# Modulation columns in blocks of 2,048 with 128 rows to a load, the first ones by pairs of channel blocks, and routing of three tiles placed one tile earlier

## The chip, the cores and the metric

One NeuronCore of a Trainium2 chip runs the whole kernel. The metric is device time in microseconds (us) from launch to end. PE is the matmul engine (TensorE), PEld its weight loads, DVE is VectorE, ACT is ScalarE, POOL is GpSimd, SP is SyncE, which here only issues DMAs. Everything is fp32 or fp32r (an fp32 pair of high and low part).

## The reference, cut to what matters

A two-layer transformer for 256 tokens x and 256 context tokens, width D = 1024. Each layer starts from a modulation: six vectors of 1,024 per condition (two conditions: c for the tokens, c_ctx for the context), from one matrix product with a weight of 1024 x 6144 per layer.

```
for layer in range(2):
    m = split(silu(cond) @ ada_w[layer] + ada_b[layer], 6)    # for c and for c_ctx
    hx = rmsnorm(x, norm_mix_g) * (1 + m[1]) + m[0]           # the same for ctx
    layer 0: even_mixer (projections, four gated-scan heads, gelu gating, output projection)
    layer 1: mla_mixer  (latent attention)
    x   = x + m[2] * mixer(hx, hc)
    h2  = rmsnorm(x, norm_ffn_g) * (1 + m[4]) + m[3]
    x   = x + m[5] * hier_moe(h2)       # top-1 group, top-2 of 8 experts in it, 32 experts
return rmsnorm(x, final_g)
```

The first two vectors of layer 0 (m[0] and m[1]) are wanted at once; the other ten are wanted later: m[2] to m[5] of layer 0 at the end of its mixer, those of layer 1 after the first MoE.

## The kernel before, in words

The program has four stages one after the other: the even layer (0 to about 393 us of the span), the MoE of layer 0 (to about 890), the odd layer (to about 1085) and the MoE of layer 1. In both MoE stages 192 loads of 1 MB each bring the expert weights through a ring of buffers; PE works through two experts a `step`.

The even layer runs nine matrix products of 512 tokens x 1024 x 512, each of 96 fp32r matmuls of 512 columns on PE (L120 to L122, called from `proj`, `head_proj` and the output loop). In order: a first `proj` (with `modulated` making its input), `head_proj` for heads 0 to 3, each overlapped with the scan `gla` of the head before, two more `proj` (the gating halves, overlapped with the last `gla` and with `gelu`), then the output product in two halves. The first half is the loop at L757 to L765; the second half is the loop over four token tiles at L790 to L807. Each tile of the second half ends with `residual`, `R.tile(t)` (transposes L213, router logits L217, their scaling L218), and `R.rows(t)` (normalised rows, L234 on DVE, L235 on POOL, `split` on ACT and DVE). `R.route` (L240 to L308) picks groups and experts from the logits in some forty small DVE operations; it is called for tiles 0 to 2 and for tile 3, both at t == 3. Between the halves, `R.fold` (L174 to L194) folds modulation vectors into the router weights; it reads them back from DRAM with DMAs that ACT issues (L179).

The modulation is done in 24 chunks of 512 columns (`ada_chunk`), each from two loads of 512 rows x 512 columns, 1 MB each, in rows of 2 KB (`ada_load`, `load`, L330). A chunk is 32 matmuls: 8 row blocks k times 4 column tiles j; column tile j writes 32 output partitions, with 128 columns of the weight moving. fp32 takes two instructions a matmul, so L404 counts 64 a chunk. The bias comes in with 4 more (8 instructions of 128 columns, L412), then one copy (L417) or one DVE operation with the norm gain (L415), and four small DMAs on POOL's queue into the DRAM tensor `mod` (L419). Chunks 0 to 3 (m[0], m[1] of layer 0) are not written to `mod`; they are transposed (L409) into columns `cols` by `first_cols`, two chunks for channel blocks 0 to 3 and two for 4 to 7. The other 20 are strewn over the even layer from the list `todo`: `between` calls `ada_next` after k = 4 and 6 of the first product and after k = 1 and 4 of each later one; the output loop does so at L764; `while adaq` (L808) takes what is left. Each call processes one chunk and issues the loads of the next into `wpb` (two buffers); one chunk is loaded into `wpa` (L786).

The order of instructions within an engine is not the order of the source: a scheduler works it out before the run from modelled times and from the source order as priority, so a chunk of L404 is cut in pieces between other PE work. On the chip each engine takes its queue strictly in order. `nc.sync` is SP's DMA queue, `nc.scalar` ACT's, `nc.gpsimd` POOL's; a DMA that waits for a buffer holds up what stands behind it in its queue.

Of the kernel before, what the change touches and what calls it, by code (L numbers as in the profile page):

```python
# [11 lines left out]
OP = mybir.AluOpType  # L12
# [13 lines left out]
def body(ctx, tc, I, out, dbg=None, stop=None):  # L26
# [310 lines left out]
    def even_layer(HL, main):  # L337
# [6 lines left out]
        with ExitStack() as st:  # L344
# [41 lines left out]
            gain = ap.tile([128, 3, 2, 128], F32, name="gain")  # L386
            V.memset(gain, 0.0)
            gains = {(1, 1): 0, (0, 4): 1, (1, 4): 2}
            for (l, g), i in gains.items():
                src = I["norm_mix_g" if g == 1 else "norm_ffn_g"][l]  # L390
                for j in range(4):
                    nc.gpsimd.dma_start(gain[32 * j:32 * j + 2, i], bass.AP(tensor=src.tensor, offset=src.offset + j * 128,
                                                                            ap=[[0, 2], [512, 2], [1, 128]]))

            def ada_load(l, c, pool):
                return load(I["ada_w"][l][:, c * 512:(c + 1) * 512], pool, nc.gpsimd if l and c >= 12 else nc.sync)

            def ada_chunk(l, c, w, cols=None):

                g, half = divmod(c, 2)  # L400
                pa = P("ad")
                for k in range(KC):
                    for j in range(4):
                        mm(pa[32 * j:32 * j + 32, 0:128], cst[:, k, :], w[k // 4][:, k % 4, j * 128:(j + 1) * 128],  # L404
                           start=k == 0, stop=cols is not None and k == KC - 1, skip_group_check=True)
                r = ap.tile([128, 128], F32, name="ada_r", bufs=2)
                if cols is not None:
                    act(r, pa[:, 0:128], AF.Copy)
                    tp(cols[:, c, :], r, ident)  # L409
                    return  # L410
                for j in range(4):
                    mm(pa[32 * j:32 * j + 2, 0:128], sbi[:, l * 12 + c, :], adab[:, j * 128:(j + 1) * 128],  # L412
                       start=False, stop=True, skip_group_check=True)
                if (l, g) in gains:
                    V.scalar_tensor_tensor(r, pa[:, 0:128], 1.0, gain[:, gains[l, g], half], op0=OP.add, op1=OP.mult)  # L415
                else:
                    act(r, pa[:, 0:128], AF.Copy)  # L417
                for j in range(4):
                    nc.gpsimd.dma_start(mod[l, g, :, half * 512 + j * 128:half * 512 + (j + 1) * 128],  # L419
                                        r[32 * j:32 * j + 2, :])  # L420

            hH = [HL.tile([128, KC, 256], F32R, name=f"hH{c}") for c in range(2)]
            hL = [HL.tile([128, KC, 256], F32R, name=f"hL{c}") for c in range(2)]

            first, w0 = {}, []
            for hf in range(2):
                for g in range(2):
                    first[2 * g + hf] = ada_load(0, 2 * g + hf, wpb if (hf, g) == (1, 0) else rp)
                w0 += load(W_in[hf * 512:(hf + 1) * 512, 2048:2560], wpa)
# [7 lines left out]
            for k in range(KC):  # L437
                p = P("mm")
# [5 lines left out]
                else:  # L444
                    V.tensor_copy(raw[k], p)
            pcol = P("bt", (128, 4, 128))
            cols = [ep.tile([128, 2, 4, 2], F32, name=f"cols{hf}") for hf in range(2)]

            def first_cols(hf):

                for g in range(2):
                    ada_chunk(0, 2 * g + hf, first[2 * g + hf], pcol)
                    V.tensor_tensor(cols[hf][:, g], pcol[:, 2 * g + hf].rearrange("p (b x) -> p b x", x=32)[:, :, 0:2],
# [1017 lines left out]
```

## Time and profile before

| What | Value |
|---|---|
| Median of 3 runs | 1577.54 us (1573.78 to 1579.67) |
| The profiled execution, its own time | 1578.11 us |
| Its span, first to last instruction | 1576.1 us |
| PE busy | 1452.8 us, 92% of the span |
| DVE, ACT, POOL busy | 41%, 27%, 16% |
| Mean DMA rate over the span | 314 GB/s |
| Mean granted clock of PE | 0.968 |

The profile shows one execution. A digit string cuts the span in 40 slices of 39.4 us and gives the busy share in tenths. Busy time of an engine is the union of its instructions; PE's ends are modelled and overlap, so a busy PE is not a PE at its peak. A wait is told with the instruction that ended it. "x64" is a count of instructions, not of source calls.

### The profile page before, as it was taken

What the parts mean: (1) busy time and instruction counts of PE and PEld (TensorE: products, weight loads), DVE (VectorE), ACT (ScalarE), POOL (GpSimd) and SP (SyncE); (2) the same over time, 40 slices, a digit from 0 to 9 for tenths busy, and PEclk for the clock granted to TensorE, in tenths of its full rate; (3) what the DMA queues carried; (4) which work ended last, traced back from release to release, by engine and by line L of the source; (5) the groups of instructions that cost most, each with busy time, mean ns of one, the idle gap of its engine ahead of it and who ended that gap; (6) DMA issues with size and microseconds to landing.
All of it is one profiled execution on the core that took longest, in us unless ns stands there. A gap on an engine that the chain in (4) does not pass through costs nothing. (4 is left out here: it accounts for less than half of the span.)

```text
span 1576.1 us, 21582 instructions
## 1 busy us (share of the span) xinstructions
PE 1452.8 (92%) x8526; PEld 822.1 (52%) x8526; DVE 646.1 (41%) x1476; ACT 432.4 (27%) x984; POOL 249.3 (16%) x272
## 2 busy tenths in 40 slices
PE   6999999998999999999999888997999998988997
PEld 5777777866444444543535356876344433333332
DVE  4555556758214323233322445576232322221323
ACT  4443334523111121121111134454122212211211
POOL 2321212133002202112203301002010200010111
PEclk9999999998999999999999989998999999999999
DMA  9774434885999999999899663125999999999995
GB/s 352 218 248 154 139 130 161 294 321 187 373 409 402 409 403 395 409 401 405 330 401 378 253 253 99 51 100 201 386 409 409 408 409 409 408 409 409 409 409 218
DMA packets 174179, 495.22 MB, mean 314 GB/s; under 512 B 17723, under 2 KB 38636, under 8 KB 174072
## 3 DMA queue, kind: packets, MB, share of 16 engines
q1 hardware_dynamic: 167832, 487.33, 80.9%
q10 hardware_dynamic: 2192, 3.72, 0.6%
q0 software_dynamic: 4048, 2.73, 0.6%
q8 instruction: 70, 1.15, 0.3%
q14 instruction: 37, 0.30, 0.1%
HBM read 492.59 MB, written 1.13 MB: 313 GB/s over the span
## 5 line engine op out<-in xcount | busy, mean ns | idle before, releaser
L921 PE MATMUL gu<-w,xT 128*64 128x512 f32 x2048 | 463.5, 600 | 26.4 <-DMA w<-in_moe_w_gu_dram 21.5
L921 PEld LDWEIGHTS gu<-w,xT 128*64 128x64 f32 x2048 | 150.3, 138 | 327.7 <-issue 272.6
L1037 PE MATMUL dn<-w,hT 128*64 128x512 f32 x960 | 226.7, 608 | 1.9 <-DMA w<-in_moe_w_dn_dram 1.5
L1056 POOL TENSOR_TENSOR xx<-xx,z 128x512 f32<-128x512 f32 x64 | 82.9, 1308 | 775.2 <-DVE z L1055 775.2
L929 DVE COPY hh<-gu 128x256 f32<-128x256 f32 x64 | 27.2, 425 | 373.6 <-ACT he L928 373.6
L1037 PEld LDWEIGHTS dn<-w,hT 128*64 128x64 f32 x960 | 69.0, 139 | 138.4 <-issue 128.9
L928 ACT ACTIVATE he<-gu 128x256 f32<-128x256 f32 x64 | 24.5, 383 | 406.6 <-PE gu L921 406.6
L1052 PE MATMUL ad<-y,PT 128*128 128x512 f32 x360 | 100.0, 417 | 20.0 <-DVE z L1055 19.9
L120 PE MATMUL mm<-WH,hH 128*128 128x512 f32 x288 | 117.1, 409 | 1.2 <-ACT hH L115 1.2
L121 PE MATMUL mm<-WL,hH 128*128 128x512 f32 x288 | 115.2, 401 | 1.4 <-DVE WL L116 1.4
L122 PE MATMUL mm<-WH,hL 128*128 128x512 f32 x288 | 112.2, 399 | 0.0
L1042 DVE SCALAR_TENSOR_TENSOR y<-dn,ws,y 128x512 fp32r<-128x512 f32 x60 | 45.1, 751 | 139.6 <-ACT y L1041 137.6
L1052 PEld LDWEIGHTS ad<-y,PT 128*128 128x128 f32 x360 | 64.7, 192 | 56.3 <-DVE z L1055 29.8
L1041 ACT ACTIVATE y<-dn,ws 128x512 fp32r<-128x512 f32 x60 | 41.2, 687 | 185.8 <-PE dn L1037 181.9
L1055 DVE TENSOR_TENSOR z<-ad,gt 128x512 f32<-128x512 f32 x96 | 65.7, 689 | 62.8 <-POOL xx L1056 38.3
L116 DVE TENSOR_TENSOR WL<-w,WH 128x512 fp32r<-128x512 f32 x76 | 56.6, 752 | 55.2 <-ACT WH L115 54.6
L115 ACT ACTIVATE WH<-w 128x512 fp32r<-128x512 f32 x80 | 48.5, 627 | 109.6 <-PE mm L122 89.0
L404 PE MATMUL ad<-w,cst 128*32 128x128 f32 x1536 | 60.5, 285 | 5.7 <-DMA w<-in_ada_w_dram 5.6
L120 PEld LDWEIGHTS mm<-WH,hH 128*128 128x128 f32 x288 | 55.2, 192 | 17.5 <-issue 4.0
L419 POOL DMA_DIRECT2D mod<-ada_r x80 | 40.4, 512 | 141.6 <-ACT ada_r L417 127.9
L121 PEld LDWEIGHTS mm<-WL,hH 128*128 128x128 f32 x288 | 55.2, 192 | 13.3 <-DVE WL L116 1.5
L122 PEld LDWEIGHTS mm<-WH,hL 128*128 128x128 f32 x288 | 54.1, 189 | 13.0 <-issue 1.6
(439 smaller groups left out, 1946.3 us busy)
## 6 DMA issues: line engine op xcount, KB each, us to landing
w<-in_moe_w_gu_dram SPq DMA_DIRECT2D x256, 1024.0 KB, 16.3
w<-in_moe_w_dn_dram SPq DMA_DIRECT2D x120, 1024.0 KB, 11.5
w<-in_ada_w_dram SPq DMA_DIRECT2D x48, 1024.0 KB, 7.4
w<-in_ev_w_in_dram SPq DMA_DIRECT2D x32, 256.0 KB, 4.3
w<-in_moe_w_dn_dram SPq DMA_DIRECT2D x16, 512.0 KB, 11.3
w<-in_ev_w_in_dram SPq DMA_DIRECT2D x6, 1024.0 KB, 5.0
w<-in_ev_w_out_dram SPq DMA_DIRECT2D x4, 1024.0 KB, 6.8
w<-in_od_w_out_dram SPq DMA_DIRECT2D x4, 1024.0 KB, 5.0
```

Source lines behind the costliest of these rows:

```text
L115: act(H, src, AF.Copy)
L116: (eng or V).tensor_tensor(L, src, H, op=OP.subtract)
L120: mm(out, lh, rh, start=start, stop=False, skip_group_check=True)
L121: mm(out, lh, rl, start=False, stop=False, skip_group_check=True)
L122: return mm(out, ll, rh, start=False, stop=stop, skip_group_check=True)
L404: mm(pa[32 * j:32 * j + 32, 0:128], cst[:, k, :], w[k // 4][:, k % 4, j * 128:(j + 1) * 128], start=k == 0, stop=cols is not None and k == ...
L921: mm(gu[64 * c:64 * c + 64, :], xT[:, k, base:base + CAP], w[:, c], start=k == 0, stop=k == KC - 1)
L1037: mm(py[c][64 * par:64 * par + 64, :], hT[par][:, k // 2, k % 2, :], w_[par][:, k % 2, c * 512:(c + 1) * 512], start=k == 0, stop=k == 3)
L1042: V.scalar_tensor_tensor(y[c][:, 1], py[c], ws, y[c][:, 0], op0=OP.mult, op1=OP.subtract)
L1052: mm(cb, PT[:, t, :], y[c][:, i % 2], start=i == 0, stop=i == 2 * len(pend) - 1)
L1055: V.tensor_tensor(z, cb, gate[t // 2][:, hs_], op=OP.mult)
L1056: nc.gpsimd.tensor_tensor(xs[t][:, hs_], xs[t][:, hs_], z, op=OP.add)
```

## The change

Three parts, all in the even layer.

1. The modulations other than the first two are made in five blocks of 2,048 columns (two vectors each) instead of 20 chunks of 512. A block has four parts (`ada_part`), each of two loads of 128 rows x 2,048 columns (1 MB each, rows of 8 KB). A part is 8 matmuls, 4 column tiles of 512 moving columns for each of 2 row blocks (16 instructions), that go on summing in one PSUM bank over the four parts; the fourth part adds the bias (8 instructions of 512 columns) and makes one copy and four DMAs. There are again 20 parts of 2 MB. `between` calls them after k = 6 of the first product and k = 1, 3 and 6 of each later one.
2. The first two vectors are made in four units of two channel blocks (256 columns of each vector) instead of two of four blocks; each unit has four loads of 512 KB in rows of 1 KB. The normalised transposes (`raw_block`, before L437 to L445) are no longer all ahead of it: blocks 0 to 3 come first, 4 to 7 between the units, and they use the PSUM tag `bt`.
3. `R.route(0, 3)` is called at t == 2 instead of t == 3.

```diff
-            gain = ap.tile([128, 3, 2, 128], F32, name="gain")
+            gain = ap.tile([128, 2, 512], F32, name="gain")
...
+            def first_load(u, pool):
+                ws = []
+                for i in range(2):
+                    w = pool.tile([128, 4, 2, 256], F32, name="w")
+                    for g in range(2):
+                        c0 = g * D + 256 * u
+                        mark["load"] = nc.sync.dma_start(w[:, :, g], I["ada_w"][0][i * 512:(i + 1) * 512, c0:c0 + 256]
+                                                         .rearrange("(k p) n -> p k n", p=128))
+                    ws.append(w)
+                return ws
+            def first_unit(w, pc):
+                pa = P("ad")
                 for k in range(KC):
                     for j in range(4):
+                        mm(pa[32 * j:32 * j + 32, 0:128], cst[:, k, :], w[k // 4][:, k % 4, j // 2, (j % 2) * 128:(j % 2 + 1) * 128],
+                           start=k == 0, stop=k == KC - 1, skip_group_check=True)
...
+                act(r, pa[:, 0:128], AF.Copy)
+                tp(pc, r, ident)
+            def ada_load(l, q, i, pool):
+                ws = []
+                for k in (2 * i, 2 * i + 1):
+                    w = pool.tile([128, 2048], F32, name="w")
+                    mark["load"] = nc.sync.dma_start(w, I["ada_w"][l][k * 128:(k + 1) * 128, q * 2048:(q + 1) * 2048])
+                    ws.append(w)
+                return ws
+            def ada_part(l, q, i, w):
+                if i == 0:
+                    bank[0] = P("ad")
+                pa = bank[0]
+                for kk in range(2):
+                    for j in range(4):
+                        mm(pa[32 * j:32 * j + 32, :], cst[:, 2 * i + kk, :], w[kk][:, j * 512:(j + 1) * 512],
+                           start=i + kk == 0, stop=False, skip_group_check=True)
+                if i < 3:
                     return
                 for j in range(4):
+                    mm(pa[32 * j:32 * j + 2, :], sbi[:, l * 12 + 4 * q + j, :], adab, start=False, stop=True, skip_group_check=True)
+                r = ap.tile([128, 512], F32, name="ada_r", bufs=1)
+                if (l, q) in gains:
+                    p0, n = gains[l, q]
+                    V.scalar_tensor_tensor(r[p0:p0 + 64], pa[p0:p0 + 64], 1.0, gain[p0:p0 + 64, n], op0=OP.add, op1=OP.mult)
+                    act(r[64 - p0:128 - p0], pa[64 - p0:128 - p0], AF.Copy)
                 else:
+                    act(r, pa, AF.Copy)
                 for j in range(4):
+                    nc.gpsimd.dma_start(mod[l, 2 * q + j // 2, :, (j % 2) * 512:(j % 2 + 1) * 512], r[32 * j:32 * j + 2, :])
...
+            w0 = []
+            first = [first_load(0, rp)]
+            w0 += load(W_in[0:512, 2048:2560], wpa)
+            first += [first_load(1, rp), first_load(2, wpb)]
+            w0 += load(W_in[512:1024, 2048:2560], wpa)
+            first.append(first_load(3, rp))
...
             def modulated(k):
-                if k % 4 == 0:
-                    first_cols(k // 4)
+                if k == 0:
+                    for i in range(4):
+                        raw_block(i)
+                    first_cols(0)
+                elif k in (2, 4):
+                    raw_block(k + 2)
+                    raw_block(k + 3)
+                if k % 2 == 0 and k < 6:
+                    first_cols(k // 2 + 1)
...
-            todo = [(0, c) for c in range(4, 12)] + [(1, c) for c in range(12)]
+            todo = [(l, q, i) for l, q in ((0, 1), (0, 2), (1, 0), (1, 1), (1, 2)) for i in range(4)]
...
-                if k in ((4, 6) if first else (1, 4)) and adaq:
+                if k in ((6,) if first else (1, 3, 6)) and adaq:
                     ada_next()
...
-                if t == 3:
+                if t == 2:
                     R.route(0, 3)
+                elif t == 3:
                     R.route(3, 4)
```

## Rows read from the trace of the kernel before

**Rows 1.** The page's slices of PE and of the DMA engines.

```profile
PE   6999999998999999999999888997999998988997
...
DMA  9774434885999999999899663125999999999995
```

**Rows 2.** Stretches 405 to 410 and 430 to 500 us: busy per engine, clock, DMA share, GB/s.

```profile
405.00:410.00 5.00, 5.00 (x26) 1.69 (x24) 0.97 (x4) 0.00 (x0) 0.00 (x0) 1.00 0.72 228
430.00:500.00 70.00, 67.23 (x344) 31.11 (x342) 21.93 (x38) 12.60 (x29) 10.37 (x8) 1.00 1.02 405
```

**Rows 3.** PE's waits from 60 to 342 us: total, times, longest.

```profile
PE ad L404 <- DMA w<-in_ada_w_dram: 4.2, 4, 2.3
```

**Rows 4.** L404 alone by stretch: PE busy (instructions), PEld busy, clock, DMA.

```profile
60.00:287.00 227.00, 31.00 (x768) 21.38 (x768) 0.99 0.53 169
287.00:334.00 47.00, 8.06 (x192) 5.65 (x192) 1.00 0.86 310
```

**Rows 5.** L412 (the bias) alone in the first of these stretches.

```profile
60.00:287.00 227.00, 4.95 (x96) 1.22 (x96) 0.99 0.53 169
```

**Rows 6.** PE's timeline around one chunk that runs almost whole.

```profile
191.23 1.74 PE L404 MATMUL ad<-w,cst 128*32 128x128 f32 x56
192.90 0.40 PE L412 MATMUL ad<-adab,sbi 24*2 24x128 f32 x8
193.22 0.50 PE L120 MATMUL mm<-WH,hH 128*128 128x512 f32 x1
```

**Rows 7.** The chain that ended last: expert products, two column tiles of 64, 512 columns.

```profile
1259.74 13.97 PE gu L921 x64
```

**Rows 8.** PE's timeline before the first product.

```profile
27.67 0.33 PE L409 MATMUL bt<-ident,ada_r 128*128 128x128 f32 x1 [1.76 <-ACT ada_r L408]
...
29.66 0.80 PE L120 MATMUL mm<-WH,hH 128*128 128x512 f32 x1 [0.49 <-ACT hH L115]
```

**Rows 9.** DVE's timeline at the end of the first product.

```profile
59.20 0.69 DVE L518 COPY sg<-mm 128x512 f32<-128x512 f32 x1 [1.98 <-PE mm L122]
```

**Rows 10.** Stretches with loads in rows of 2 KB, then of 512 B (columns as in 2).

```profile
16.00:36.00 20.00, 17.27 (x244) 14.29 (x244) 11.01 (x27) 8.01 (x19) 0.00 (x0) 0.91 1.05 383
144.50:147.50 3.00, 3.00 (x24) 2.23 (x26) 2.29 (x4) 0.88 (x2) 0.00 (x0) 1.00 0.93 266
```

**Rows 11.** Four loads of 256 KB (L477), issued 142.5 to 144.0 us.

```profile
DMA to landing us min/median/max: 3.7/4.3/4.5
```

**Rows 12.** ACT's timeline at the end of the output product's first half.

```profile
330.48 0.28 ACT L417 ACTIVATE ada_r<-ad 128x128 f32<-128x128 f32 x1 [3.25 <-PE ad L412]
```

**Rows 13.** DVE's timeline there.

```profile
335.53 1.12 DVE L187 TENSOR_TENSOR wA<-wr,rcol 128x320 f32<-128x320 f32 x2 [7.75 <-DMA rcol<-mod]
```

**Rows 14.** PE's timeline from there to the second half's first products.

```profile
334.65 1.95 PE L404 MATMUL ad<-w,cst 128*32 128x128 f32 x64
...
342.94 0.60 PE L121 MATMUL mm<-WL,hH 128*128 128x512 f32 x1 [1.37 <-DVE WL L116]
```

**Rows 15.** PE's timeline at the end of the even layer.

```profile
371.18 1.98 PE L217 MATMUL bt<-wA,h2T 128*128 128x40 f32 x16
...
374.04 1.28 PE L404 MATMUL ad<-w,cst 128*32 128x128 f32 x34
...
380.26 1.52 PE L404 MATMUL ad<-w,cst 128*32 128x128 f32 x32 [1.44 <-DMA w<-in_ada_w_dram]
381.71 3.64 PE L217 MATMUL bt<-wA,h2T 128*128 128x40 f32 x16
...
403.19 1.08 PE L921 MATMUL gu<-w,xT 128*64 128x512 f32 x4
```

**Rows 16.** DVE's timeline there.

```profile
380.19 0.26 DVE L218 SCALAR_TENSOR_TENSOR lg<-bt,rs_y,bS 128x40 f32<-128x40 f32 x1
...
385.39 0.26 DVE L218 SCALAR_TENSOR_TENSOR lg<-bt,rs_y,bS 128x40 f32<-128x40 f32 x1 [0.73 <-PE bt L217]
...
392.44 1.22 DVE L861 TENSOR_TENSOR P<-iota,cm 128x1024 fp32r<-128x1024 f32 x1
```

More of the change, by code (lines that the diff above doesn't have):

```diff
@@ L385, in even_layer @@
             nc.gpsimd.dma_start(adab, I["ada_b"].rearrange("l (c n) -> (l c) n", n=512))
-            gain = ap.tile([128, 3, 2, 128], F32, name="gain")
+            gain = ap.tile([128, 2, 512], F32, name="gain")
             V.memset(gain, 0.0)
[L388 to L400, printed above, removed]
+            gains = {(1, 0): (64, 0), (0, 2): (0, 0), (1, 2): (0, 1)}
+            for (l, q), (p0, i) in gains.items():
+                src = I["norm_ffn_g" if q else "norm_mix_g"][l]
+                for j in range(2):
+                    nc.gpsimd.dma_start(gain[p0 + 32 * j:p0 + 32 * j + 2, i], bass.AP(tensor=src.tensor, offset=src.offset + j * 512,
+                                                                                      ap=[[0, 2], [1, 512]]))
+            def first_load(u, pool):
[9 more added lines that the diff above has]
+            def first_unit(w, pc):
                 pa = P("ad")
@@ new lines, in first_unit @@
+                r = ap.tile([128, 512], F32, name="ada_r", bufs=1)[:, 0:128]
+                act(r, pa[:, 0:128], AF.Copy)
[7 more added lines that the diff above has]
+                return ws
@@ L416, in ada_chunk @@
                 else:
-                    act(r, pa[:, 0:128], AF.Copy)
+                    act(r, pa, AF.Copy)
                 for j in range(4):
-                    nc.gpsimd.dma_start(mod[l, g, :, half * 512 + j * 128:half * 512 + (j + 1) * 128],
-                                        r[32 * j:32 * j + 2, :])
+                    nc.gpsimd.dma_start(mod[l, 2 * q + j // 2, :, (j % 2) * 512:(j % 2 + 1) * 512], r[32 * j:32 * j + 2, :])
+            bank = [None]
             hH = [HL.tile([128, KC, 256], F32R, name=f"hH{c}") for c in range(2)]
@@ L423, in even_layer @@
             hL = [HL.tile([128, KC, 256], F32R, name=f"hL{c}") for c in range(2)]
[L425 to L429, printed above, removed]
+            w0 = []
+            first = [first_load(0, rp)]
+            w0 += load(W_in[0:512, 2048:2560], wpa)
+            first += [first_load(1, rp), first_load(2, wpb)]
@@ L436, in even_layer, with raw_block @@
                 V.tensor_scalar(dg[:, t, :], ident, rstd_of(xs[t], D, 1.0 / D, dg0), None, op0=OP.mult)
-            for k in range(KC):
-                p = P("mm")
+            def raw_block(k):
+                p = P("bt")
                 for t in range(4):
```

34 lines of the change are left out of this document (13 added, 21 removed).

## The prediction

> **What bounds the kernel now.** I read the page's slices first. PE is nearly full all along, and the DMA engines are full in two stretches only [rows 1]: slices 11 to 22 and 29 to 40, the two MoE stages. From 40 to 315 us their digits are 3 to 8 while PE's are 9. So the even layer is PE's and each MoE stage the DMA engines'. The reader is to see that nothing in the MoE stages changes, and that all that can change is when the even layer lets the first of them begin.
>
> Then the windows view, to see whether an earlier beginning is worth anything. In 430 to 500 us the DMA share is 1.02 at 405 GB/s: the expert weights set the pace. But in 405 to 410 us the share is 0.72 [rows 2]: the ring of buffers is full and the loads wait until PE, which began its first expert product at 403.19 [rows 15], gives a buffer back. What the even layer gains or loses therefore moves all that follows by as much, and I make the sum on the position of that product.
>
> Then the waits of PE from 60 to 342 us: four waits for modulation weights, 4.2 us together [rows 3]. PE's own work sets the order there, so each us added to PE between 60 and 287 us is a us on the path. Last, the timelines of three places in which PE does wait: the start, the seam between the two halves of the output product, and the end of the layer.
>
> **The change, part by part.**
>
> *A chunk's price now.* In 60 to 287 us, 768 instructions of L404, which are 12 chunks, keep PE busy for 31.00 us, and their bias for 4.95 [rows 4, 5]: 2.99 us a chunk. A chunk that runs nearly whole takes 193.22 - 191.23 = 1.99 [rows 6]. So about 1 us of a chunk's price comes from its being cut up among other products.
>
> *A part's price.* The trace has no product of four column tiles with 512 columns moving. The nearest is the expert product: two column tiles, 512 columns, 64 instructions in 13.97 us [rows 7], 218 ns each. With four tiles side by side, as L404 has them, I estimate half of that, 109 ns: 16 instructions make 1.75 us, and the bias (8 instructions for four parts) 0.22 a part. That is 1.97, the whole chunk's 1.99 again: the columns are the same in number, so the wide tile by itself gains nothing, and only cutting can be saved. Below: 1.97, never cut. Above: 2.99, cut as now. I take 2.5, halfway, since 16 long instructions offer fewer seams than 72 short ones, but the work that cuts in is the same.
>
> *Heads and the two later products, 60 to 287 us: +9 us.* By the new places, heads take 12 parts and the two products 6, 18 in place of 12 chunks: 18 x 2.5 = 45 for 12 x 2.99 = 36. Between 18 x 1.97 = 35.5 (nothing) and 18 x 2.99 = 53.8 (+18). Their copies (5 in place of 20) and their POOL DMAs (20 for 80) hide behind PE as they did. Each part still needs 2 MB, at 405 GB/s some 5.2 us, in two buffers that come free only when the part before is done; behind such a load in SP's queue stand the head weights. Three parts in a stage stand two or three row blocks apart (24 or 36 products) and mostly more, with a scan between.
>
> *The start: -5 us.* First loads of x and ctx (2.1 MB), two chunks (4.2 MB) and 1 MB of W_in now stand before the first product, which starts at 29.66 [rows 8]. After: one unit, so 2.1 MB less, at 383 GB/s [rows 10] 5.5 us. PE's wait of 1.76 for ACT, which was copying weights, may go too: -7.3 at best. Against it, units come in rows of 1 KB. The trace has rows of 2 KB (383 GB/s at share 1.05, so 365 at a full share) and of 512 B (266 at 0.93, so 286) [rows 10]. All 8.4 MB at 286 would take 29.4 us in place of 23: the last unit 6.4 us later, which eats the lead, since the last quarter of the product waits for it. So -7.3 to 0 for the product's end, at 59.2 now [rows 9]; 1 KB lies between the two rates, and raw blocks 4 to 7 fill PE's waits: I take -5. The product holds one modulation piece at its end before and after.
>
> The Trainium skill ("DMA: Bandwidth & Descriptors") asks for loads of at least 1 MiB (section Measured (HBM→SBUF, 128 partitions, SWDGE, issued from GpSimd)) and gives one DMA about 2.0 us plus bytes / 436e3 (section Anatomy of one DMA — SWDGE (gpsimd) path). If loads followed one another by that formula, 16 of 512 KB would take, by estimate, 51 us where 8 of 1 MB take 35, and the kernel would come out 16 us later than my sum. The trace speaks against loads following one another.
>
> *The output product's first half and the seam: -6 us.* In 287 to 334 us three chunks run, 192 instructions of L404 [rows 4], 8.06 and some 1.2 of bias, 9.3 us. One part remains (2.5). At the seam, ACT stood 3.25 us before a chunk's copy at 330.48, waiting for PE's bias [rows 12], and the DMA that reads `mod` back for the fold is behind that copy in ACT's queue; DVE then stood 7.75 for it to land [rows 13]. PE filled the time with two whole chunks from 334.65 on and still waited 1.37 for the split weights at 342.94 [rows 14]. With no chunk there, the fold's DMA goes at least 3.25 sooner; the cover for the two chunks was free, so taking them out gives nothing itself. At most the seam moves by the 6.8 us taken from PE in front. I take 6: the third chunk's pieces stood ahead of the transposes that end the gating. Bounds 3 to 7.
>
> *The end: -5 us.* The last tile's logits were ready at 385.39 on DVE, waiting for L217 [rows 16]. Ahead of that L217 on PE stood a piece of a chunk at 374.04 (with its bias 1.5 us), a wait of 1.44 for weights and a piece of 1.45 [rows 15]: 4.4 us that go. It also took 3.64 where that of another tile took 1.98 [rows 15]. From the third tile's logits (380.19) to the one-hots (392.44) DVE has 12 us of work, both routes and a split [rows 16]. Routing three tiles earlier lets that start before the last tile's logits. If DVE's 12 us were simply full, only the 1.5 us would be won; if all went, 7. I take 5. Late next would be the last tile's normalised rows (DVE, POOL, ACT, DVE in turn), which now share DVE with a route that has priority. No DMA is moved with the route; the expert loads behind the last chunks on SP go sooner, but into a ring that is full before PE starts anyway.
>
> *Sum.* -5 + 9 - 6 - 5 = -7. From the profiled execution's 1578.1: 1571 us; its time is 0.6 above the median of 1577.5, so the median is about as good a start.
>
> **Rivals.**
>
> *A, the sum*, 1571, with its own range 1562 to 1578. Chance 0.52.
>
> *B, uncut parts.* If the scheduler leaves parts whole, the heads cost nothing more: 1571 - 9 = 1562. For it: one chunk in the heads does run whole [rows 6]. Against: most are cut, or 12 would not cost 36. It comes out lower still if the start gives 7. Chance 0.14.
>
> *C, the shift gives all back.* Parts cost what chunks cost: +18 in place of +9, so 1580. Six pieces move from places where PE waited anyway (seam, end) into the stretch in which it doesn't, and nothing is earned by that. Chance 0.13. Here too belongs that the expert loads are behind at the start and swallow the lead, 1578; against it the 0.72 [rows 2]; 0.04.
>
> *D, PE waits for modulation weights in the heads: slower.* Three parts a stage on one pair of buffers, each load let go only by the part before. Now 4 waits take 4.2 us over the 12 chunks [rows 3], the longest 2.3. If each of 18 parts waited 1.2 more, that would be +22: 1593. It decides from 0.85 us a part, where the 15 us between my sum and slower by 0.5% are used up. For it: SP's strict order and 6 MB in place of 4 a stage. Against: from 60 to 287 us the DMA share is 0.53 at 169 GB/s [rows 4]. Chance 0.12.
>
> *E, first loads one after another*: the 16 half-size loads of the start, if each took its landing time alone. Four loads of 256 KB issued over 1.5 us landed 3.7 to 4.5 us after their issue [rows 11]; one behind another they would have needed four times 3.7. By the shortest landing 16 loads would take 59 us, some 30 more than the bytes, of which PE's other work hides half: about 1586. Chance 0.05. The skill's formula above gives 1587 for the same course.
>
> **How the numbers follow.** 0.5% is 7.9 us, about what a measurement of this kernel can tell from no change; faster is below 1569.6, slower above 1585.4. My point lies just inside. Of A's 0.52, about 0.32 falls below 1569.6, since four terms each uncertain by some 4 us spread the sum by about 8; all of B is faster: 0.46. The rest of A, and C, are the same: 0.37. D and E are slower: 0.17. Reaching down through B to 1558 and up past C to 1585 leaves out D and E and little else, under 2 in 10.
>
> **What would show each step.** Parts: L404's successor busy per part in the heads, 2.5 (B: 2.0; C: 3.0); the stretch from the first product's end to the last gating product's, longer by about 9. Start: first product near 24 to 25, its end near 54. Seam: no modulation work between the halves, the fold's DMA issued before 330, the second half starting about 3 to 6 sooner after the first. End: no modulation work behind the second half's products; from the third tile's logits to the one-hots below 10 us. D: waits of the modulation products for their DMA above 20 us in total. The MoE stages should be as long as before. The prediction is wrong if the first expert product moves by 7 and the end doesn't, or if the heads' stretch moves by more than 18.

## The result and the profile after

The changed kernel takes 1586.38 us (median of 7, 1583.88 to 1593.51) where the kernel before takes 1577.54 in the same comparison: ratio 1.008, 95% interval 1.0051 to 1.011. It is slower by 0.8% by that ratio (the two medians alone stand 0.56% apart); 1571 was forecast, in a range of 1558 to 1585. The profiled execution spans 1584.6 us in place of 1576.1, so its own difference is +8.5.

The page's slices of the changed kernel, first row PE, then the clock granted to PE, then the DMA engines, say that the balance is the old one ([rows 1]): the two MoE stages are the DMA engines', the even layer is PE's.

```profile
PE   7999999986799999999999888997999989988997
...
PEclk9999999997899999999999899997999999999999
DMA  9885455853799999999899863225999999999995
```

So the reckoning is made as in the prediction, on positions in the even layer. I cut it at four instructions that both kernels have: the first matmul of head 0, the last of the seventh product, the third tile's logits on DVE, the one-hots on DVE (the matrix P with which the gather picks its rows).

| stretch | before | after | difference | forecast |
|---|---|---|---|---|
| start, to head 0's first matmul | 63.45 | 58.90 | -4.6 | -5 |
| heads and the two later products | 237.35 | 247.75 | +10.4 | +9 |
| output's first half and seam, to the third tile's logits | 79.39 | 77.04 | -2.4 | -6 |
| end, to the one-hots | 12.25 | 18.46 | +6.2 | -5 |
| gather, to the first expert product | 10.75 | 10.63 | -0.1 | 0 |
| all behind it | 1172.9 | 1171.8 | -1.1 | 0 |

The differences add up to +8.4, the span's +8.5. Two lines are right, one gave less than half, and the end went the other way by 11 us. That one is most of the error. (Of the end's -5, the 1.5 for the piece at 374.04 in [rows 15] belong by their place to the line above: that piece stood ahead of the third tile's logits.)

PE's timeline of the changed kernel at its first product and at these cuts (start, length, instruction, what it waited for; [rows 8, 15] answer to the first and last of them), then the kernel before at the two cuts that its rows don't show:

```profile
25.66 0.50 PE L120 MATMUL mm<-WH,hH 128*128 128x512 f32 x1
...
58.90 0.50 PE L120 MATMUL mm<-WH,hH 128*128 128x512 f32 x1
...
306.65 0.39 PE L122 MATMUL mm<-WH,hL 128*128 128x512 f32 x1
...
412.78 1.08 PE L963 MATMUL gu<-w,xT 128*64 128x512 f32 x4
```

```profile
63.45 0.39 PE L120 MATMUL mm<-WH,hH 128*128 128x512 f32 x1
...
300.80 0.39 PE L122 MATMUL mm<-WH,hL 128*128 128x512 f32 x1
```

**The end.** PE's timeline of the changed kernel behind the second half's products, then DVE's ([rows 15, 16] answer to them):

```profile
382.60 1.05 PE L217 MATMUL bt<-wA,h2T 128*128 128x40 f32 x4
392.30 0.21 PE L282 MATMUL bt<-Mb,before 128*128 128x32 bf16 x1 [8.64 <-DVE Mb L274]
392.40 1.94 PE L213 MATMUL bt<-ident,w 128*128 128x128 f32 x8
...
394.31 3.61 PE L217 MATMUL bt<-wA,h2T 128*128 128x40 f32 x16
```

```profile
383.69 0.26 DVE L218 SCALAR_TENSOR_TENSOR lg<-bt,rs_y,bS 128x40 f32<-128x40 f32 x1 [1.07 <-PE bt L217]
...
397.97 0.26 DVE L218 SCALAR_TENSOR_TENSOR lg<-bt,rs_y,bS 128x40 f32<-128x40 f32 x1 [3.19 <-PE bt L217]
...
402.15 1.23 DVE L903 TENSOR_TENSOR P<-iota,cm 128x1024 fp32r<-128x1024 f32 x1
```

Read the order in PE's queue, not the durations. L282 is the rank product of the route of tiles 0 to 2 (it counts each token's place in its expert's list); it needs their one-hot mask Mb, the end of a chain on DVE. It now stands ahead of L213 and L217, the last tile's transposes and logits, which need nothing from that route. PE stands 8.64 us at it with the last tile's work behind it. So its logits come at 397.97, 12.6 us later than in [rows 16], and the second route begins only then: the two routes, which shared DVE before, run one behind the other, with DVE idle for 3.19 us between.

**The heads.** The windows of the two kernels over that stretch (sum of PE, weight loads, DVE, ACT and POOL busy, clock, DMA share, GB/s), first the kernel before, then the changed one; then the changed one's modulation products L435 and bias L440 alone:

```profile
63.50:300.80 237.30, 232.40 (x1925) 180.04 (x1924) 135.95 (x290) 92.02 (x177) 57.43 (x76) 0.99 0.56 182
```

```profile
58.90:306.60 247.70, 246.85 (x1376) 163.75 (x1373) 135.63 (x274) 95.14 (x173) 41.24 (x40) 1.00 0.62 213
...
58.90:306.60 247.70, 48.17 (x284) 7.82 (x280) 1.00 0.62 213
...
58.90:306.60 247.70, 4.14 (x32) 0.41 (x32) 1.00 0.62 213
```

A part is 16 instructions. Four of the 284 belong to a piece that starts at 57.91 and reach in with their modelled ends only; 280 are 17.5 parts: (48.17 + 4.14) / 17.5 = 2.99 us a part, just what a chunk cost, 2.99 [rows 4, 5]. Why so much, PE's timeline shows, around a part that runs whole, around one that is cut within a row, and around half a part with the bias behind it:

```profile
123.13 1.92 PE L435 MATMUL ad<-w,cst 128*32 128x512 f32 x16
124.98 0.50 PE L120 MATMUL mm<-WH,hH 128*128 128x512 f32 x1
...
148.07 1.04 PE L435 MATMUL ad<-w,cst 128*32 128x512 f32 x2
149.04 0.66 PE L721 MATMUL bt<-ident,o 128*128 128x128 f32 x4
...
150.96 1.92 PE L435 MATMUL ad<-w,cst 128*32 128x512 f32 x14
152.81 0.50 PE L122 MATMUL mm<-WH,hL 128*128 128x512 f32 x1
...
323.21 1.06 PE L435 MATMUL ad<-w,cst 128*32 128x512 f32 x8
324.21 1.03 PE L440 MATMUL ad<-adab,sbi 24*2 24x512 f32 x8
```

Sixteen records took 1.85 from start to next start; 2 took 0.97 and the other 14 again 1.85; 8 took 1.00. A pair of records is one matmul in one column tile, eight records are one row of four tiles side by side, and a lone tile takes as long as all four. The Trainium skill ("TensorE: Matmul & The Clock Gate", section Measured speedup vs the span model) says the same from the other end: a pack lasts about one matmul and some 4 ns for each further tile; here 0.97 for one tile and 1.00 for eight records. So a cut within a row costs a whole row more, 0.97, where a whole row of a chunk takes 0.24 ([rows 6]: 56 records, seven rows, in 1.67).

**The first half.** PE's waits of the changed kernel from 58.9 to 306.6 us, then from 306.6 to 345, then of the kernel before from 300.8 to 334.3 (total, times, longest); [rows 3] answers to the first:

```profile
PE ad L435 <- DMA w<-in_ada_w_dram: 0.8, 2, 0.5
...
PE mm L120 <- ACT hH L115: 4.4, 2, 3.3
PE bt L792 <- DVE gv L789: 1.8, 1, 1.8
...
PE ad L404 <- DMA w<-in_ada_w_dram: 0.5, 1, 0.5
PE mm L120 <- ACT hH L115: 0.4, 1, 0.4
```

The waits for modulation weights are nearly gone. But in the output product's first half PE now waits 6.2 us for the gated half of the input, where the kernel before waited 0.4 for it and 0.5 for weights. Its timeline there with the gating products, those of the kernel before, and the window behind the wait:

```profile
317.95 1.95 PE L775 MATMUL bt<-gv,wsT 128*128 128x128 f32 x16
...
322.65 0.63 PE L792 MATMUL bt<-ident,gv 128*128 128x128 f32 x4 [1.76 <-DVE gv L789]
...
329.13 0.79 PE L120 MATMUL mm<-WH,hH 128*128 128x512 f32 x1 [3.30 <-ACT hH L115]
```

```profile
301.03 1.95 PE L734 MATMUL bt<-gv,wsT 128*128 128x128 f32 x16
```

```profile
329.00:335.00 6.00, 5.87 (x16) 4.70 (x17) 3.41 (x7) 1.51 (x5) 0.62 (x2) 0.50 0.23 89
```

The gating products of the last two tiles (L775) stand at 317.95, behind four row blocks of the output product; in the kernel before they ran at 301.03, right behind the seventh product. And after the wait the granted clock is 0.50 for 6 us, its lower level: the 96 products of this half take 24.8 us in place of 22.9.

### The profile page after: what moved, and what is told of

The parts are those of the page before. It is cut to its first block, busy times and chain, and to the rows that moved or that the text cites. A ratio compares the mean times of both kernels' runs of the same rounds, so it can differ in the third digit from the quotient of the medians.

```text
span 1584.6 us, 19309 instructions
## 1 busy us (share of the span) xinstructions
PE 1452.2 (92%) x7446; PEld 791.6 (50%) x7446; DVE 650.4 (41%) x1475; ACT 433.3 (27%) x975; POOL 218.1 (14%) x206
## 5 line engine op out<-in xcount | busy, mean ns | idle before, releaser
L120 PEld LDWEIGHTS mm<-WH,hH 128*128 128x128 f32 x288 | 54.7, 190 | 35.0 <-issue 12.1
L122 PEld LDWEIGHTS mm<-WH,hL 128*128 128x128 f32 x288 | 54.4, 190 | 14.6 <-issue 3.1
L928 PE MATMUL ad<-P,hH 128*128 128x256 f32 x256 | 52.9, 289 | 1.8 <-DVE P L903 1.8
L435 PE MATMUL ad<-w,cst 128*32 128x512 f32 x320 | 53.2, 603 | 0.8 <-DMA w<-in_ada_w_dram 0.8
## 6 DMA issues: line engine op xcount, KB each, us to landing
w<-in_ev_w_in_dram SPq DMA_DIRECT2D x6, 1024.0 KB, 10.4
```

What stands on the lines that cost most here:

```text
L120: mm(out, lh, rh, start=start, stop=False, skip_group_check=True)
L122: return mm(out, ll, rh, start=False, stop=stop, skip_group_check=True)
L435: mm(pa[32 * j:32 * j + 32, :], cst[:, 2 * i + kk, :], w[kk][:, j * 512:(j + 1) * 512], start=i + kk == 0, stop=False, skip_group_check=True)
L928: mm(px[:, j, :], hs[t][:, part, 128 * k:128 * k + 128], P[:, t, :], start=i == 0, stop=i == 2 * NT - 1)
```

## The experiments

Each kernel was timed beside the kernel before on one chip, in groups (e1 to e4, e5 to e8, e9 to e12, e13 and e14) on a chip each. A profiled execution can lie some us off the median of its kernel (that of the route back is 8.5 below it and the fastest of its six runs), so totals are read from the ratios and the causes from positions within the traces.

| kernel | ratio to before | 95% interval | first expert product | third tile's logits to one-hots |
|---|---|---|---|---|
| changed kernel | 1.0080 | 1.0051 to 1.011 | +9.6 | 18.5 |
| e1 route back | 1.0044 | 1.0031 to 1.0058 | +3.1 | 12.3 |
| e2 route alone | 1.0026 | 1.0010 to 1.0042 | +3.0 | 16.0 |
| e3 rank late | 1.0043 | 1.0025 to 1.0061 | +3.5 | 12.3 |
| e4 pairs alone | 0.9981 | 0.9963 to 0.9999 | -3.1 | 11.4 |
| e5 places alone | 1.0027 | 1.0009 to 1.0046 | -0.1 | 12.3 |
| e6 width, old places | 1.0111 | 1.0088 to 1.0134 | +12.3 | 14.6 |
| e7 whole rows, new places | 1.0021 | 1.0004 to 1.0039 | -0.2 | 12.1 |
| e8 whole rows, old places | 1.0020 | 1.0003 to 1.0038 | +1.7 | 15.0 |
| e9 pairs and places | 1.0018 | 0.9998 to 1.0037 | +3.3 | 12.3 |
| e10 weights late | 1.0006 | 0.9986 to 1.0025 | -1.2 | 11.4 |
| e11 addition on DVE | 0.9969 | 0.9955 to 0.9982 | -8.8 | 10.9 |
| e12 both | 0.9972 | 0.9954 to 0.9991 | -7.6 | 9.4 |
| e13 gate buffers | 1.0025 | 1.0007 to 1.0043 | +3.2 | 12.3 |
| e14 all mended | 0.9981 | 0.9964 to 0.9997 | -7.4 | 12.6 |

**The route, from three sides.** e1 takes it back in the changed kernel, e2 puts it alone into the kernel before, e3 keeps its DVE work early and moves only its rank products behind the last tile:

```
                 rstd = R.tile(t)
-                if t == 2:
+                if t == 3:
                     R.route(0, 3)
-                elif t == 3:
                     R.route(3, 4)
```

```
                 if t == 2:
-                    R.route(0, 3)
+                    R.route(0, 3, rank=False)
                 elif t == 3:
+                    R.rank(0, 3)
                     R.route(3, 4)
```

> The changed kernel with the route of tiles 0 to 2 back behind the last tile's logits. Theory Q (PE's fixed order): in the changed kernel the rank product L282 of tiles 0 to 2, which waits for DVE's one-hots, stands in PE's queue ahead of the last tile's transposes L213 and logits L217, and so DVE's first route delays the last tile's logits. Then this kernel has the last tile's logits 8 to 13 us sooner than the changed one, the one-hots of the gather 6 to 10 us sooner, and it takes 1576 to 1580 us in place of 1586. Rival V (DVE is simply full from the third tile's logits to the one-hots, and what was lost is a slower DVE beside POOL and half clock on PE): the logits come sooner but the one-hots don't, and the time stays within 2 us of 1586.

> The kernel before with the earlier route alone. Theory Q: the rank product again stands ahead of the last tile's transposes, so the last tile's logits (385.4 in the kernel before) come 8 to 12 us later and the time is 1582 to 1587 us, nearly the whole loss of the changed kernel. Rival V: both routes are the same work on DVE in any order, no change beyond 2 us. Prediction's step: 3 to 7 us faster, 1571 to 1575.

> The changed kernel with the route of tiles 0 to 2 still at the earlier place on DVE, and only its rank products (L282, L284) and the one addition that reads them moved behind the last tile's logits. Theory Q: PE's order is mended and DVE has its first route done sooner, so the last tile's logits come as early as in the kernel with the route back, and the one-hots 0 to 4 us earlier than there: 1573 to 1580 us. Rival V (DVE's share is what delays): as slow as the changed kernel, 1584 to 1588, since DVE's order is the same.

PE's timeline with the route back, then DVE's busy time from the third tile's logits to the one-hots in e1 and in e3 (columns as in the windows above), then PE's and DVE's timelines with the route alone:

```profile
383.20 3.47 PE L217 MATMUL bt<-wA,h2T 128*128 128x40 f32 x16
392.04 0.29 PE L282 MATMUL bt<-Mb,before 128*128 128x32 bf16 x2 [5.37 <-DVE Mb L274]
```

```profile
382.60:394.90 12.30, 4.81 (x30) 4.48 (x28) 12.23 (x66) 2.36 (x6) 3.40 (x3) 0.50 0.27 85
...
383.80:396.10 12.30, 4.82 (x30) 4.49 (x28) 12.23 (x66) 2.36 (x6) 3.40 (x3) 0.50 0.27 85
```

```profile
385.72 0.19 PE L282 MATMUL bt<-Mb,before 128*128 128x32 bf16 x1 [0.83 <-DVE Mb L274]
385.75 1.95 PE L213 MATMUL bt<-ident,w 128*128 128x128 f32 x8
...
387.67 3.61 PE L217 MATMUL bt<-wA,h2T 128*128 128x40 f32 x16
...
391.32 0.26 DVE L218 SCALAR_TENSOR_TENSOR lg<-bt,rs_y,bS 128x40 f32<-128x40 f32 x1 [3.02 <-PE bt L217]
```

The queue's order decides (theory Q). With the last tile's L217 back in front of L282 its logits come at 386.9 in place of 398.0, and 6.1 us of the stretch are back, all that it had lost. The route alone costs 3.8 us there, since two chunks cover a part of PE's wait, and 0.26% in the time; its 1581.5 us lie just under the range, and its last logits came 5.9 us later, not 8 to 12. The mended order in e3 is worth as much as e1, and no more: DVE's earlier start gives nothing, because DVE is busy for 12.23 of the 12.30 us in both. That is the case for which the prediction had kept its lower bound.

The totals say less than the positions. e1's 1584.9 missed its 1576 to 1580 and e3's 1583.8 its 1573 to 1580; by its median alone e1 even lies where rival V had it, within 2 us of 1586. What excludes V is the trace: the one-hots came 7.3 us sooner. In the whole time the ratio moved by 0.36%, 5.7 us, with intervals that overlap; the clearest measure of the order is e2's 0.26%, whose interval does not reach 1.

**The start alone.** e4 is the kernel before with the diff's parts for the first units, nothing else.

> The kernel before with only the first modulations by pairs of channel blocks. Theory S (the start gives less than the prediction's 5, because the second half of the first product waits for its later units): first product 4 us sooner, its end 1 to 3 us sooner, and the same through to the end: 1574.5 to 1577. Rival: the whole 5 arrives at the end, 1572.5. Rival: the heads take it all back, 1577 to 1579.

Head 0's first matmul comes 4.0 us sooner, the first expert product 3.1, the time is 0.19% less. Its 1574.4 us lie just below theory S's range and above the rival's 1572.5, though more of the lead was there at head 0 than the 1 to 3 us of S. In e10, e11 and e12, which have the same first loads, the start gave 3.3, 4.5 and 2.4. It varies by as much without the pairs: e2, which begins as the kernel before does, has head 0 at 61.17, 2.3 us sooner (its granted clock from 30 to 60 us was 1.00, that of the kernel before 0.96), and e5, with one place fewer in the first product and no pairs, at 59.09.

**Places, width and cuts.** e5 and e9 change the places and keep chunks of 512 columns, e9 with the pairs; e6 keeps the wide parts and takes the places back; e7 and e8 put a part's eight matmuls at the scheduler's highest priority, so that nothing else cuts into a row (e8 at the old places).

```
-                if k in ((4, 6) if first else (1, 4)) and adaq:
+                if k in ((6,) if first else (1, 3, 6)) and adaq:
```

```
+                with tc.high_priority():
                     for kk in range(2):
                         for j in range(4):
                             mm(pa[32 * j:32 * j + 32, :], cst[:, 2 * i + kk, :], w[kk][:, j * 512:(j + 1) * 512],
```

> The kernel before, its chunks of 512 columns kept, at the changed kernel's places alone (one in the first product, three in each later stage). Theory W (the heads lose by the wide part, since 16 of its records are only two rows of four column tiles, and a piece that holds one tile of a row takes as long as the whole row): chunks at the new places cost at most 2.99 us each as before, so 18 for 12 is +13 to +18 before the output product, the seam gives 6 to 8 back and the end, with no chunk there, 3 to 5: 1576 to 1584 us, and the modulation work of the heads is no dearer by the piece than before. Rival P (the places are all of the loss, width none): the output product begins 12 to 16 us later, as in the changed kernel, and the time is that of the changed kernel with the route back, 1.0044 of before.

> The kernel before with the first modulations by pairs and the new places, its chunks of 512 columns and its route kept: the change without its wide parts and without the earlier route. If the terms add up, it is the 4 us of the pairs on top of the places alone (1.0027): first expert product 3 to 5 us sooner than in the kernel before, time 0.998 to 1.002 of before, 1573 to 1579 us. Rival (the pairs' 4 us are lost where the places put a third piece into every stage): no faster than the places alone, 1.0027.

> The changed kernel (wide parts, first modulations by pairs) with the places of before and the route back. Theory W: 12 parts of 2.7 to 2.8 us stand where 12 chunks of 2.8 to 3.0 did, so the heads change by -3 to 0, the start gives 3.8, and 7 parts are left for the output product and the end as 8 chunks were: 1571 to 1576 us. Rival P2 (wide parts cost more in themselves, wherever they stand): 1577 or above.

> The changed kernel with the route back and the eight matmuls of a part at the scheduler's highest priority, so that no other product cuts into a row of four column tiles; places as changed. Theory W: a row costs 1.0 us alone and two rows 1.85, so 17 parts cost 32 to 35 us and not 48, the output product begins 8 to 14 us sooner than in the changed kernel with the route back, and the time is 1566 to 1576. Rival P: the number of parts sets the price, not their cuts; the same time as with the route back. Rival D of the prediction: whole parts stand in front of products that are ready and PE waits for their weights, more than 10 us in total, 1585 or above.

> Wide parts, pairs, the route back, places of before, and the rows of four kept whole by priority. Theory W: 12 parts in the heads cost 24 in place of 33 to 36 us, the start gives 3.8, seam and end stay nearly as before: 1562 to 1569. If the seam and the end matter more than the heads, it is no faster than the kernel with whole rows at the new places.

The modulation products and their bias with whole rows, over the stretch from head 0 to the seventh product (columns as before):

```profile
60.50:302.80 242.30, 38.82 (x300) 6.12 (x296) 1.00 0.67 228
...
60.50:302.80 242.30, 6.16 (x32) 0.56 (x32) 1.00 0.67 228
```

Of the 300 instructions 296 begin in the stretch, 18.5 parts, at 44.98 us 2.43 each in place of 2.99, and more of them: the cuts within rows cost about 0.55 us a part. Chunks at the new places (e5) cost 3.00, as at the old ones, and e5's time lies where theory W had it, though not by W's path: only 15.7 chunks fell into the stretch, which grew by 4.7 us (242.0 for 237.35), and the output product began 0.3 us sooner than in the kernel before, not 13 to 18 later. The stretch from head 0 to the seventh product is 5.1 us shorter than in e1 (242.3 for 247.5), with a part more in it; 8 to 14 were expected. In the whole time the rows won 0.23% on e1, with intervals that overlap, and the 1577.1 us lie above the range, 1566 to 1576.

e9 is half a miss: its ratio of 1.0018 lies in the range, but not by the path expected, for its first expert product came 3.3 us later, not 3 to 5 sooner; beside e5, where it came 0.1 sooner, the pairs show no gain in these two traces, as the rival had it.

Steps in a row, each kernel with one part more, give the account of the whole: pairs -0.19%, then the new places +0.37% (e9 on e4), then the wide parts +0.26% (e1 on e9), then the route +0.36% (the changed kernel on e1). By the intervals each step is uncertain by 0.2 to 0.3%. At the first expert product the same steps are -3.1, +6.4, -0.2 and +6.5 us: places and route show in both measures, the wide parts in the ratio only, and with 2.99 us a part for 3.00 a chunk their cost isn't shown.

e6 was a plain miss: at the old places the wide parts are worse, 1.0111, though its heads are shorter (230.0 us in place of 247.75, and of 237.35 in the kernel before). Its time would fit rival P2, its heads don't: 12.5 parts cost 2.70 each there. Its waits between 300 and 400 us:

```profile
ACT WH L115 <- DMA gate<-mod: 11.0, 1, 11.0
...
PE ad L435 <- DMA w<-in_ada_w_dram: 8.0, 2, 6.8
```

The parts left for the seam wait for their weights behind expert loads on the full DMA engines (share 1.03 at 405 GB/s from 340 to 346 us), and the gate's DMA, on ACT's queue ahead of the split of the output weights, holds that for 11 us. This is rival D of the prediction, at another place than it looked for. e8 missed by the same stretch: its seventh product ends 10.4 us sooner than in the kernel before (290.4), but the output's first half takes 44.4 us for 33.5, with 7.1 of parts and 5.4 of waits in it, and the end 15.0. So parts with cut rows are worse at the old places than at the new (1.0111 for 1.0044), and with whole rows the places are level (1.0020 for 1.0021).

**DVE at the end.** In e10 a route returns its arithmetic of the combine weights and its rank addition, and the weights of both routes are queued on DVE behind the last of these additions, and the one-hots get the scheduler's highest priority; e11 takes the shift's addition from POOL to DVE; e12 does both. All three stand on e4.

```
-            nc.gpsimd.tensor_tensor(h2, h2, S, op=OP.add)
+            V.tensor_tensor(h2, h2, S, op=OP.add)
```

```
-                    R.route(0, 3)
-                    R.route(3, 4)
+                    late = [R.route(0, 3), R.route(3, 4)]
...
+            with tc.issue_after(late[1][1].ins):
+                for f, _ in late:
+                    f()
```

> The pairs alone, and in the even layer the arithmetic of the combine weights (the 14 or so DVE instructions of each route that don't feed the one-hots) queued on DVE behind the last rank addition. Theory F (DVE, full from the third tile's logits to the one-hots, sets the end of the layer, and neither chunks on PE nor the place of the first route do): one-hots 2 to 3 us sooner than with the pairs alone, 9.0 to 10.5 us behind the third tile's logits in place of 11.4, and 1570 to 1573 us. Rival G (PE's chunks and transposes set the end): the one-hots come no sooner than with the pairs alone.

> The pairs alone, and the addition of the modulation's shift to a tile's normalised rows (L235, 128x1024) on DVE in place of POOL. In each trace so far the DVE instruction that runs beside a POOL L235 takes 2.2 to 2.4 us and not 0.3. Theory H (DVE stands still while POOL's addition runs): DVE pays 1.2 us in place of 2.1, no DVE instruction of 2 us is left between the third tile's logits and the one-hots, these come 0.5 to 2 us sooner, and so does the end, 1572 to 1574. Rival: the long instruction is long by itself, and DVE has 1.2 us more to do: 1.2 us later.

> The pairs alone with both edits, weights late and the addition on DVE. Theory F with H: the one-hots 8 to 9.5 us behind the third tile's logits in place of 11.4, the first expert product 6 to 8 us sooner than in the kernel before, 1568 to 1572 us, faster than both kernels. Rival: the gather then waits for the last tile's split rows and nothing more than one of the two edits is won.

POOL's and DVE's timelines of e1, then DVE's of e11 at the same point:

```profile
384.46 2.35 POOL L235 TENSOR_TENSOR h<-h,rS 128x1024 f32<-128x1024 f32 x1 [8.17 <-DVE h L234]
...
384.55 2.41 DVE L254 SCALAR_TENSOR_TENSOR h<-h,io 128x120 f32<-128x120 f32 x1
```

```profile
372.81 1.21 DVE L235 TENSOR_TENSOR h<-h,rS 128x1024 f32<-128x1024 f32 x1
...
374.57 0.28 DVE L254 SCALAR_TENSOR_TENSOR h<-h,io 128x120 f32<-128x120 f32 x1
```

The same L254 takes 2.41 us beside POOL's addition and 0.28 without it. DVE paid 1.3 to 2.2 us for each of the four tiles in the kernel before and pays 1.2 now. The first expert product comes 8.8 us sooner than in the kernel before, 5.7 more than with the pairs (0.8 of that was there at the half's end, before the first of these additions), and e11, at 0.9969, beats both kernels and missed its range on the good side (1569.4 us for 1572 to 1574): the earlier tiles and the residuals behind them win too, and the third tile's logits alone came 4.5 us sooner than in e4. e10 came out as rival G had it for the one-hots, 11.4 us behind the third tile's logits as in e4, though not for G's reason: the last rank addition came 10.0 us behind those logits, in e4 11.2, but 15 of the weights' instructions still stood between it and the one-hots. Its 1577.9 us are no gain on the kernel before, and theory F's 1570 to 1573 were missed. Together with e11's edit only four stand there, and the stretch falls to 9.4; but the first expert product is no sooner than in e11. The ratios of e11 and e12 can't be told apart.

**The first half.** e13 is e1 with four buffers for the gated tiles in place of two; e14 is e1 with these, whole rows and the addition on DVE.

```
-                gv = vp.tile([128, 512], F32, name="gv", bufs=2)
+                gv = vp.tile([128, 512], F32, name="gv", bufs=4)
...
-                gu = vp.tile([128, 512], F32, name="gv", bufs=2)
+                gu = vp.tile([128, 512], F32, name="gv", bufs=4)
```

> The changed kernel with the route back and four buffers in place of two for the gated tiles, so that the output's gating doesn't wait until PE has taken the third and fourth tile of the first gating. Theory B (two buffers): the first gating's last products, at 317.4 behind four row blocks of the output product, no longer hold back the second gating, the output's transposes begin before 320 in place of 322, PE waits less than 3 us in place of 6.2 between the last gating product and the seam, the seam comes 3 us sooner, 1577 to 1582. Rival C (cover: the gating's chain on ACT and DVE is late itself and only the chunks hid it): the transposes come no sooner, the wait stays at 5 to 6 us, the time at 1.0044.

> The changed kernel with the route back, whole rows of four, the shift's addition on DVE and four gate buffers. By the terms of the runs so far: whole rows gave 0.23% on the route back, the addition on DVE 0.12 to 0.2%, the buffers 0 to 0.2%, so 0.997 to 1.001 of before, 1571 to 1578: no better than the pairs with the addition on DVE (0.9969). If the seam's 3 us come as well, 1569.

PE's waits of e13 from 264 to 346 us:

```profile
PE ad L435 <- DMA w<-in_ada_w_dram: 3.4, 2, 2.5
PE mm L120 <- ACT hH L115: 2.9, 2, 1.7
PE bt L721 <- DVE o L718: 2.5, 1, 2.5
```

The waits in the half fall from 6.2 to 2.9 and the stretch from the seventh product's last matmul to the half's end from 37.2 to 33.0 us. But the scheduler set another order ahead of it, PE waits there for weights and for the last scan, the output's first transposes come later and not sooner (327.6 us for 322 in e1), and the seam comes where it came in e1 (L190 at 343.7 for 343.5). Theory B is right about the wait and wrong about the transposes and the seam. Its 1579.2 us lie in B's range, but the intervals of e13 and e1 overlap, so a gain isn't shown. e14 at 0.9981 is as its terms had it: faster than the kernel before, not faster than e11.

## Why the prediction was wrong, point by point

*The end* failed, and with it the sign. The step read: "Routing three tiles earlier lets that start before the last tile's logits", and what the 5 us hold beyond 1.5 hung on it. It followed the route on DVE and named what would be late next there; it did not follow the route's own products into PE's queue, where they passed the last tile's transposes and logits. Shown by e1, e2 and e3: +6.2 us, all of it order. Nor was anything won by the chunk piece and the wait behind the third tile's logits: without chunks and with the route back the stretch is 12.3 us, as before, because DVE is full. The other 1.5 us belong to the seam, where no run parts them from the rest. The bounds of the step, -1.5 to -7, held no loss at all.

*The seam and the first half* had the mechanism at one end and missed it at the other. From the half's end to the third tile's logits the changed kernel is faster by 7.2 us (38.6 for 45.9), as forecast. But "the cover for the two chunks was free, so taking them out gives nothing itself" was said of the seam, and the chunks of the half itself were counted as pure gain: there, as I read the windows, they had stood in what would have been PE's gaps. Modulation work fell by 3.0 us, waits rose by 5.4, the products by 1.9 and the transposes and gating products by 0.6, so the half is 4.9 longer. What exactly delays the gated half stays open: in e13 the waits fell to 2.9 and the seam came no sooner, so the lateness begins further up.

*The heads*, +9 forecast, +10.4 measured, came out by two errors that cancel. A part cost 2.99, not 2.5: what a piece of a wide part costs was argued from fewer seams, and a cut row was not thought of. The chunk that was read as whole was not: [rows 6] shows 56 of its 64 records, and a whole one, at 60.91 in the kernel before, takes 2.21 with its bias, so the cuts made 0.8 of a chunk's price and not 1. 2.99 is the price of rival C (parts cost what chunks cost), +16 by the same count of busy time. Against it PE's waits fell by 4.1 us, from 4.9 to 0.8, which the prediction had as a risk (rival D) and not as a gain; the 1.5 us that are left are PE's other work, 194.5 for 196.1.

*The start* was right in size, -4.6 for -5, and -4.0 in e4, but with some luck: the kernel before was profiled with a late start, as e2 shows. DVE's copy was a poor mark for it, moving by 1.7 only (57.53 for [rows 9]). Rival E did not happen: the first product stood at 25.66. Nor did what the Trainium skill's formula ("DMA: Bandwidth & Descriptors", section Anatomy of one DMA — SWDGE (gpsimd) path) would give for loads that follow one another, 16 us more; the trace speaks against that course.

*That the shift passes through* was right: +9.6 at the first expert product, +8.5 at the end. In all sixteen traces that product stands between 394 and 416 us, and what is behind it takes 1168 to 1177, no longer where it stands early.

Of the cases, A, B and C are excluded by the time, D where it was put by the waits, E by the start; what happened was none of them, though C's price of a part came true. It was a wait on PE behind DVE, made by moving a route. In the chances, 0.32 of A's 0.52 was too much for what falls below 1569.6, since A's middle, 1571, lies above that.

## What to carry to other kernels

When a step is moved earlier, follow it into the queue of every engine that it uses, and ask of each of its instructions what it waits for and what independent work then stands behind it; the engine with the long chain is not where the loss shows. Work that fills another engine's waits is free only where those waits are: take it out of a gap and the gap stays, put it into a full stretch and all of it counts. Matmuls packed side by side in column tiles must be kept together by the order, or each fragment costs a whole row.

## What the runs showed of the hardware

A single column tile with 512 columns held PE for 0.97 us, eight records in four tiles for 1.00, sixteen for 1.85; I had counted by records. A DVE instruction of 0.28 us took 2.2 to 2.4 beside POOL's last 128x1024 addition, itself some 2.4 us, in eleven of the thirteen traces that have one; in e8 it was one of 128x3 elements that took 2.2, in e7 none with two inputs began beside it. One with a single input kept its 0.28 beside it (L264 at 380.48 in the kernel before, where the addition began at 380.47). The Trainium skill ("SBUF — State Buffer", section SBUF: two separate sides) has the rule: a DVE instruction with two SBUF inputs and a POOL instruction that reads SBUF exclude each other for the whole instruction of whichever began first. The trace agrees with that, start for start (384.46 on POOL, 384.55 on DVE), and e11 is what it was worth here: 5.7 us on e4 at the first expert product, in the whole time 0.12% by the ratios, whose intervals overlap. And, in the output's first half, a wait of 3.3 us was followed by 6 us at a granted clock of 0.50, the lower of the two levels, where it had been 0.98 before.
